# Turning values and keys by VectorE blocks and transfers within SBUF, in a retention and HGRN2 trunk on one core

## The chip, the cores and the metric

The kernel runs on one core of a Trainium2 chip. The metric is the device time of one execution in microseconds (us); with several runs the median is given. A profiled execution gives a trace: every instruction of the engines with its start, its duration and what released it. TensorE (PE) multiplies, with its weight loads (PEld) as a row of their own; VectorE (DVE), ScalarE (ACT) and GpSimd (POOL) do the rest, and SyncE (SP) issues DMAs from one queue that works in order.

## The reference

One decoder layer for 272 prompt positions (16 learned meta tokens and 256 tokens) and 8 decode tokens, 280 columns in all, model width 2048, everything in float32:

```
x <- LN1(alpha*x + 0.5*SwiGLU_1(x))
x <- LN2(alpha*x + (sigmoid(a_r)*o_ret + sigmoid(a_h)*o_hg) @ w_out)
x <- LN3(alpha*x + 0.5*SwiGLU_2(x))

[q_r k_r v_r g_r q_h f i_h g_h a_r a_h] = x @ w_in        # 2048 -> 10*2048
retention, 8 heads of 256:  o = ((q k^T) * D) v + decayed q S,   S_new = gamma^C S + (decayed k)^T v
HGRN2, 16 heads of 128:     o = A v + (q exp(b)) S,              S_new = exp(b_last) S + (k exp(b_last - b))^T v
outputs: y of the 256 tokens and the 8 decode tokens, and the four states
```

The decode tokens use states read from memory; the prompt starts from zero states. What matters here: activations come out of a projection with features on the 128 partitions and time along the row, whereas the products that form a state (k^T v) and the outputs (A v) need values, and for the states keys, with time on the partitions. Those arrays must be turned.

## The kernel before

The program is one long list of matmuls in four stages: the first FFN, the projection stage with the mixer, the output projection, the second FFN. A dense matmul multiplies a 128x128 weight block with 264 to 280 columns in float32r, three times per block (high and low parts of both operands). Weights come in 868 units of 8 blocks: `load` in `stream` issues one 512 KB DMA on SP (tile `raw`, line 185), ScalarE rounds it to `whi` (L188), VectorE subtracts to get `wlo` (L189). All three tiles have three buffers, so a load can be issued as soon as VectorE is through with the unit three places ahead.

The projection stage (`project`) goes over eight head pairs u = 0..7: the six groups f, q_h, i_h, q_r, k_r, v_r of pair u (32 blocks each), then the four gate groups of pair u-1. `evacuate` takes each group out of PSUM. After i_h it starts the generator `mix_hg(u)` (HGRN2, two heads), after v_r the generator `mix_ret(u)` (retention, one head of 256 as two halves c). The generators are advanced by `pump`, once after each k step of a dense group (six matmuls); `yield n` means "go on n steps later". This is how the mixer's own matmuls are placed in TensorE's order, which is written out by hand and is exactly the order of the program. The other engines and SP's queue get their order from a planner at compile time, by priority (the order of the program, weights ahead) and its own estimate of when things are ready; on the chip each works its list in order and waits where something isn't there.

The arrays that are turned, each by TensorE with a 128x128 identity, two blocks b of 128 positions per half or head, into a PSUM bank `pt` or `ptk`, from which ScalarE copies:

- in `mix_hg`: the values `v` of both heads into `vth` (L875, L879), the tile `ends` (first 16 and last 16 columns, L878), read by the state matmuls `pst` (L1024) and the outputs `po` (L1050);
- in `turned(h)` of `mix_hg`: the decayed keys `K` into `kth` (L982, L983), read by `pst`. The loads of the decode state `smh` and values `vbh` of the second head wait for the two `kth` tiles, by a one-column copy on GpSimd (`load`, `values`);
- in `mix_ret`: the values into `vtr` (L1107, L1108), which `split` divides into `vs` (high and low parts), and the rotated keys `k_r` (L1114), which go from PSUM with the decay factors into `ks` (L1129, L1130). `tails` collects the last 24 columns of keys and values and is turned as one block (L1116). `ks` and `vs` are read by the state matmuls `psr` (L1168), `vtr` later by the outputs `por` (L1226) after `centre` has taken off its mean over the 256 features.

`samples(h)` in `mix_hg` updates the decode states on ScalarE and VectorE (L998, L999) and stores them (L1002).

`mix_ret` is started three steps after v_r for all pairs but the second:

```
start(mix_ret(c0 // 2, st["q_r"], st["k_r"], v), 24 if c0 == 2 else 3)
```

The tile `v` has one buffer; `smr` has four, shared by `ks`, `vs` and the decode states of retention.

Of the kernel before, what the change touches and what calls it, by code (L numbers as in the profile page):

```python
# [18 lines left out]
P = 128  # L19
# [109 lines left out]
def trunk(ctx: ExitStack, tc: tile.TileContext, A, O):  # L129
# [417 lines left out]
    with tc.tile_pool(name="yp", bufs=1) as yp:  # L547
# [7 lines left out]
        with tc.tile_pool(name="mp", bufs=1) as mp:  # L555
# [73 lines left out]
            def project(groups):  # L629
                for grp in groups:  # L630
# [4 lines left out]
                    if grp[0] == (QKV_ORDER[0], 0):  # L635
                        outs = norm1.first(block, outs, x0s)
                    elif grp[0] == (QKV_ORDER[2], 0):
                        v = st["i_h"] = tmp("v", (P, 2, T))
                        outs = norm1.second(block, outs, x0s, (v[:, 0, :], v[:, 1, :]))
# [8 lines left out]
            def evacuate(n, c0, c1, o0, o1, b0, b1):  # L648
# [14 lines left out]
                elif n == "i_h":  # L663
                    v = st.pop("i_h", None)
                    if v is None:
                        v = tmp("v", (P, 2, T))
                        nc.scalar.copy(v[:, 0, :], o0)
                        nc.scalar.copy(v[:, 1, :], o1)

                    start(mix_hg(c0 // 2, st["f"], st["k"], st["q"], v), {0: 20, 2: 46}.get(c0, 4))  # L670
                elif n in ("q_r", "k_r"):
                    sc, w, x0 = (1.0, TL, NMETA) if n == "q_r" else (KSC, T, 0)
                    r = tmp(n, (P, 2, w))
                    for j, (a, b, op) in enumerate(((cos, sin, ALU.subtract), (sin, cos, ALU.add))):
# [5 lines left out]
                        nc.vector.tensor_tensor(out=r[:, j, :], in0=r[:, j, :], in1=t, op=op)  # L680
                    st[n] = r
                elif n == "v_r":
                    v = tmp("v", (P, 2, T))
                    nc.scalar.copy(v[:, 0, :], o0)
                    nc.scalar.copy(v[:, 1, :], o1)
                    start(mix_ret(c0 // 2, st["q_r"], st["k_r"], v), 24 if c0 == 2 else 3)
# [24 lines left out]

            NB2 = LP - 2 * P
# [8 lines left out]
            def upper_upper_lower(out, x, at=0):  # L721
# [3 lines left out]
                sub(out[64 : 64 + n], x, out[at : at + n].bitcast(F32))  # L725

# [19 lines left out]
            def mix_hg(u, f, k, q, v):  # L746

                calm = 2
                ends = tmp("ends", (P, 2, 2, NMETA))
                nc.gpsimd.tensor_copy(ends[:, :, 0, :], v[:, :, :NMETA])  # L750
                nc.gpsimd.tensor_copy(ends[:, :, 1, :], v[:, :, T - NMETA :])
# [13 lines left out]
                def load(h):  # L765
# [3 lines left out]
                    nc.gpsimd.tensor_copy(sms[h][:, 0, :1], kts[0][:, 0, :1] if h else acc[:, 15:16])  # L769
                    nc.sync.dma_start(sms[h], A["sg"][2 * u + h])  # L770

                def values(h):
                    nc.gpsimd.tensor_copy(vbs[h][:, 0, :1], kts[1][:, 0, :1] if h else acc[:, 2 * P + 15 : 2 * P + 16])
# [95 lines left out]
                vt = tmp("vth", (P, 2, 2, P))  # L869
                vrow = []  # L870
                for h in range(2):

                    pt = mx_bank("pt")
                    for b in range(2):
                        nc.tensor.transpose(pt[:, b * P : (b + 1) * P], v[:, h, NMETA + b * P : NMETA + (b + 1) * P], ident)  # L875
                    x = pt[:64, 2 * P : 3 * P]
                    if h:
                        nc.tensor.transpose(x, ends.rearrange("p c a t -> p (c a t)"), ident)  # L878
                    nc.scalar.copy(vt[:, h], pt[:, : 2 * P].rearrange("p (b f) -> p b f", b=2))  # L879
                    if h:  # L880
# [95 lines left out]
                def turned(h):  # L976
                    kt = tmp("kth", (P, 2, P), bufs=2)
                    kts.append(kt)
                    pt = mx_bank("ptk")
                    for b in range(2):  # L980
                        t0 = NMETA + b * P
                        nc.tensor.transpose(pt[:, b * P : (b + 1) * P], K[:, h, t0 : t0 + P], ident)  # L982
                    nc.scalar.copy(kt, pt[:, : 2 * P].rearrange("p (b f) -> p b f", b=2))  # L983
# [34 lines left out]
                for h in range(2):  # L1018
# [4 lines left out]
                    for b in range(2):  # L1023
                        nc.tensor.matmul(pst[:, (b + 1) * P : (b + 2) * P], kts[h][:, b, :], vt[:, h, b, :], start=True, stop=True)  # L1024
# [21 lines left out]
                def outputs(h):  # L1046
                    po = mx_bank("po")
                    for b in range(2):
                        o = po[:, b * P : (b + 1) * P]
                        nc.tensor.matmul(o, vt[:, h, b, :], acc[:, (2 * h + b) * P : (2 * h + b + 1) * P], start=True, stop=False)  # L1050
# [26 lines left out]
            def centre(x):  # L1077

                np_, n = x.shape[0], x.shape[1]
                m = tmp("cen", (P, n))[:np_]  # L1080
                nc.vector.tensor_reduce(out=m, in_=x, op=ALU.add, axis=mybir.AxisListType.X)
                nc.vector.tensor_scalar(out=m, in0=m, scalar1=1.0 / 256, scalar2=None, op0=ALU.mult)
                nc.vector.tensor_tensor(out=x, in0=x, in1=m.unsqueeze(2).to_broadcast([np_, n, 256]), op=ALU.subtract)

            def mix_ret(u, q, k, v):
                vt = tmp("vtr", (P, 2, 2, P))

                ks, vs = (tmp(n, (P, 2, 2, 2 * P), dt=F32R, bufs=4, tag="smr") for n in ("ks", "vs"))
# [13 lines left out]
                for i, x in enumerate((k, v)):  # L1102
                    nc.gpsimd.tensor_copy(tails[:, 2 * i : 2 * i + 2, :NB], x[:, :, 2 * P :])
                for c in range(2):
                    pt = mx_bank("pt")
                    for b in range(2):
                        nc.tensor.transpose(pt[:, b * P : (b + 1) * P], v[:, c, b * P : (b + 1) * P], ident)  # L1107
# [4 lines left out]
                    pt = mx_bank("pt")  # L1112
# [264 lines left out]
```

## Time and profile before

| | |
|---|---|
| median of 3 runs | 2566.79 us (2566.35 to 2567.9) |
| profiled execution, span from first to last instruction | 2563.9 us |
| TensorE busy, granted clock | 2553.4 us, 1.000 |
| VectorE busy | 1702.8 us |
| ScalarE busy | 1392.2 us |
| GpSimd busy | 57.0 us |
| DMA engines of SP's queue | 62.0% of 16 engines' span |

The profiled execution's own time is its span; the runs' times hold some 2.9 us more around it. A line of a timeline reads: start, duration, engine, line, operation, output<-inputs, count, and in brackets the idle time before it and what ended that. A line of a group reads: line, engine, operation, shapes, count | busy us, mean ns of one | idle time before them, and what ended it. "L226" or "L240" is the line of a helper that many callers share.

### The profile page before, as it was taken

The page shows a single profiled execution, that of the slowest core. Times are in us where ns is not written, and L with a number is a line of the kernel's source. Part 1 is how long each engine was busy: PE and PEld are TensorE (multiplying, and loading weights), DVE is VectorE, ACT ScalarE, POOL GpSimd, SP SyncE. Part 2 cuts the span into 40 slices and gives each one's busy share as a digit, 9 for nine tenths or more (in the row PEclk, how much of TensorE's full clock was granted, in tenths as well). Part 3 has the DMA queues.
Part 4 walks back from the last instruction along what each step waited for, and adds up shares of the span by engine and source line. Part 5 has one row for each costly group of instructions (what it writes and reads, how often), then busy time and mean ns, then how long its engine had stood idle before and what let it go on. Part 6 is the DMA issues. An engine that isn't in the chain of part 4 may idle for free.

```text
span 2563.9 us, 56275 instructions
## 1 busy us (share of the span) xinstructions
PE 2553.4 (100%) x23424; PEld 2534.4 (99%) x23424; DVE 1702.8 (66%) x2827; ACT 1392.2 (54%) x2186; POOL 57.0 (2%) x152
## 2 busy tenths in 40 slices
PE   9999999999999999999999999999999999999999
PEld 9999999999999999999999999999999999999998
DVE  6444544475569878777777777777885555556555
ACT  5444444444456767767676666675564444444443
POOL 0000000000000000000000000000000000000000
PEclk9999999999999999999999999999999999999999
DMA  7555555555555876767676767675556565565554
GB/s 244 183 187 183 187 182 184 186 182 186 184 201 180 287 265 232 264 214 260 212 264 215 259 223 255 224 239 188 196 190 197 194 197 195 194 196 195 195 195 149
DMA packets 156897, 536.26 MB, mean 209 GB/s; under 512 B 17952, under 2 KB 25952, under 8 KB 156640
## 3 DMA queue, kind: packets, MB, share of 16 engines
q1 hardware_dynamic: 156352, 532.37, 62.0%
q8 instruction: 183, 3.00, 0.5%
q14 instruction: 74, 0.61, 0.1%
q10 hardware_dynamic: 288, 0.29, 0.0%
HBM read 501.99 MB, written 30.61 MB: 208 GB/s over the span
## 4 chain that ended last, share of the span: by engine, by line
PE 96%; DVE 2%; ACT 0%; issue 0%; DMA 0%; SPq 0%; ACTq 0%; DVEq 0%
PE up L218 36%; PE dn L218 19%; PE pj_i_h L218 3%; PE pj_g_r L218 3%; PE pj_q_h L218 3%; PE pj_g_h L218 3%; PE pj_a_r L218 3%; PE pj_a_h L218 3%; PE pj_f L218 3%; PE pj_q_r L218 3%; PE pj_k_r L218 3%; PE wo L218 3%; PE pj_v_r L218 3%; DVE wlo L189 1%; PE pqr L1211 1%; PE psr L1168 0%
## 5 line engine op out<-in xcount | busy, mean ns | idle before, releaser
L189 DVE TENSOR_TENSOR wlo<-raw,whi 128x1024 fp32r<-128x1024 f32 (+1 forms) x869 | 1062.2, 1223 | 740.7 <-ACT whi L188 737.3
L188 ACT CAST whi<-raw 128x1024 fp32r<-128x1024 f32 (+1 forms) x870 | 905.7, 1042 | 909.2 <-PE up L218 411.0
L218 PE MATMUL up<-xh,whi 128*128 128x280 f32 (+1 forms) x2624 | 725.6, 280 | 0.6 <-ACT whi L188 0.6
L218 PE MATMUL up<-xh,wlo 128*128 128x280 f32 (+1 forms) x2624 | 725.8, 280 | 0.4 <-DVE wlo L189 0.3
L218 PE MATMUL up<-xl,whi 128*128 128x280 f32 (+1 forms) x2624 | 725.4, 279 | 0.0
L218 PEld LDWEIGHTS up<-xh,wlo 128*128 128x128 f32 x2624 | 492.6, 189 | 1.0 <-DVE wlo L189 1.0
L218 PEld LDWEIGHTS up<-xh,whi 128*128 128x128 f32 x2624 | 492.6, 189 | 0.8 <-ACT whi L188 0.8
L218 PEld LDWEIGHTS up<-xl,whi 128*128 128x128 f32 x2624 | 492.6, 189 | 0.0
L218 PE MATMUL dn<-hh,whi 128*128 128x280 f32 (+1 forms) x1376 | 384.7, 280 | 0.0
L218 PE MATMUL dn<-hh,wlo 128*128 128x280 f32 (+1 forms) x1376 | 384.3, 279 | 0.0
L218 PE MATMUL dn<-hl,whi 128*128 128x280 f32 (+1 forms) x1376 | 384.3, 279 | 0.0
L218 PEld LDWEIGHTS dn<-hh,whi 128*128 128x128 f32 x1376 | 260.1, 189 | 0.1
L218 PEld LDWEIGHTS dn<-hl,whi 128*128 128x128 f32 x1376 | 260.1, 189 | 0.1
L218 PEld LDWEIGHTS dn<-hh,wlo 128*128 128x128 f32 x1376 | 260.1, 189 | 0.0
L218 PE MATMUL pj_k_r<-xh,whi 128*128 128x280 f32 x256 | 74.2, 290 | 0.0
L218 PE MATMUL pj_g_r<-xh,whi 128*128 128x264 f32 x256 | 74.0, 289 | 0.0
L218 PE MATMUL pj_v_r<-xh,whi 128*128 128x280 f32 x256 | 73.8, 288 | 0.0
L218 PE MATMUL pj_v_r<-xh,wlo 128*128 128x280 f32 x256 | 72.4, 283 | 0.3 <-DVE wlo L189 0.3
L218 PE MATMUL pj_g_h<-xh,whi 128*128 128x264 f32 x256 | 72.7, 284 | 0.0
L218 PE MATMUL pj_k_r<-xh,wlo 128*128 128x280 f32 x256 | 72.4, 283 | 0.0
L218 PE MATMUL pj_v_r<-xl,whi 128*128 128x280 f32 x256 | 72.3, 283 | 0.0
L218 PE MATMUL pj_k_r<-xl,whi 128*128 128x280 f32 x256 | 72.3, 283 | 0.0
(421 smaller groups left out, 5263.4 us busy)
## 6 DMA issues: line engine op xcount, KB each, us to landing
raw<-in_w_up SPq DMA_DIRECT2D x343, 512.0 KB, 4.1
raw<-in_w_in SPq DMA_DIRECT2D x320, 512.0 KB, 4.3
raw<-in_w_dn SPq DMA_DIRECT2D x172, 512.0 KB, 3.5
smr<-in_sr SPq DMA_DIRECT2D x32, 512.0 KB, 5.0
out_srs<-smr SPq DMA_DIRECT2D x32, 512.0 KB, 6.7
raw<-in_w_out SPq DMA_DIRECT2D x32, 512.0 KB, 3.9
vbr<-vrd SPq DMA_DIRECT2D x32, 256.0 KB, 4.1
smh<-in_sg SPq DMA_DIRECT2D x16, 512.0 KB, 5.2
```

Of the source, the lines that this page charges most:

```text
L188: nc.scalar.copy(hi[:, j:jn, :], raw[:, j:jn, :])
L189: nc.vector.tensor_tensor(out=lo[:, j0:j1, :], in0=raw[:, j0:j1, :], in1=hi[:, j0:j1, :].bitcast(F32), op=ALU.subtract)
L218: nc.tensor.matmul(o, w, t, start=start, stop=stop)
L1211: nc.tensor.matmul(pq[32 * j : 32 * j + 32, :256], qdr_at[c][:, 32 * b : 32 * b + 32], sms[2 * e + c][:, j, :], start=e + c == 0, stop=e + ...
```

## The change

The 128 TensorE transposes of `v` (both branches), `k_r` and `K` are replaced. VectorE's `transpose` turns each 32x32 block of a 128x256 operand in place within its 32 partitions, straight from PSUM for i_h and v_r; `pieces` chooses where the blocks lie in the scratch tile. Then `turned_over` moves block (i, j) of a 4x4 grid to (j, i) with 16 DMAs on SP's queue, each of 32 partitions with 512 bytes a row (256 for K). The scratch tile is `v` for i_h, k_r and v_r, and the dead tile `k` for K. The turned tiles are laid out feature by feature with half and block inside (`TURNED`, step of four floats between neighbouring features; `kth` has a step of two).

`evacuate` now fills `ends` and the values' part of `tails` from PSUM by ScalarE, where GpSimd copied them from `v`. `ks` is allocated and filled when k_r is evacuated, and its decay and split read it from SBUF instead of PSUM. `centre` reduces over two dimensions for the new layout. The yields are as before.

```diff
+            TURNED = (P, P, 2, 2)
+            def pieces(z, c):
+                return z[:, :, c].rearrange("p (i f) b -> p b i f", i=4)
+            def turned_over(out, z):
+                z, out = (x.rearrange("p f c b -> p (f c b)") for x in (z, out))
+                n = z.shape[1] // 4
+                for j in range(4):
+                    for i in range(4):
+                        nc.sync.dma_start(
+                            out[32 * j : 32 * j + 32, n * i : n * (i + 1)], z[32 * i : 32 * i + 32, n * j : n * (j + 1)])
...
                 elif n == "i_h":
-                    v = st.pop("i_h", None)
-                    if v is None:
-                        v = tmp("v", (P, 2, T))
-                        nc.scalar.copy(v[:, 0, :], o0)
-                        nc.scalar.copy(v[:, 1, :], o1)
+                    ends = tmp("ends", (P, 2, 2, NMETA))
+                    vt = tmp("vth", TURNED)
+                    v = tmp("v", TURNED)
+                    for j, o in enumerate(st.pop("i_h", (o0, o1))):
+                        nc.vector.transpose(pieces(v, j), o[:, NMETA:LP])
+                        nc.scalar.copy(ends[:, j, 0, :], o[:, :NMETA])
+                        nc.scalar.copy(ends[:, j, 1, :], o[:, T - NMETA : T])
+                    turned_over(vt, v)
...
+                    if n == "k_r":
+                        st["ks"] = ks = tmp("ks", (P, 2, *TURNED[1:]), dt=F32R, bufs=4, tag="smr")
+                        z = tmp("v", TURNED)
+                        for j in range(2):
+                            nc.vector.transpose(pieces(z, j), r[:, j, : 2 * P])
+                        turned_over(ks[:, 1].bitcast(F32), z)
...
                 elif n == "v_r":
-                    v = tmp("v", (P, 2, T))
-                    nc.scalar.copy(v[:, 0, :], o0)
-                    nc.scalar.copy(v[:, 1, :], o1)
+                    vt = tmp("vtr", TURNED)
+                    v = tmp("v", TURNED)
+                    for j, o in enumerate((o0, o1)):
+                        nc.vector.transpose(pieces(v, j), o[:, : 2 * P])
+                        nc.scalar.copy(tails[:, 2 + j, : T - 2 * P], o[:, 2 * P :])
+                    turned_over(vt, v)
...
                 def turned(h):
-                    kt = tmp("kth", (P, 2, P), bufs=2)
+                    kt = tmp("kth", (P, P, 1, 2), bufs=2)
                     kts.append(kt)
-                    pt = mx_bank("ptk")
-                    for b in range(2):
-                        t0 = NMETA + b * P
-                        nc.tensor.transpose(pt[:, b * P : (b + 1) * P], K[:, h, t0 : t0 + P], ident)
-                    nc.scalar.copy(kt, pt[:, : 2 * P].rearrange("p (b f) -> p b f", b=2))
+                    z = k[:, h, : 2 * P].rearrange("p (f c b) -> p f c b", c=1, b=2)
+                    nc.vector.transpose(pieces(z, 0), K[:, h, NMETA:])
+                    turned_over(kt, z)
...
                 for c in range(2):
-                    pt = mx_bank("pt")
+                    f = slice(c * P, (c + 1) * P)
                     for b in range(2):
-                        nc.tensor.transpose(pt[:, b * P : (b + 1) * P], v[:, c, b * P : (b + 1) * P], ident)
-                    nc.scalar.copy(vt[:, :, c, :], pt[:, : 2 * P].rearrange("p (b f) -> p b f", b=2))
-                    f = slice(c * P, (c + 1) * P)
-                    split(vs[:, 0, :, f], vs[:, 1, :, f], vt[:, :, c, :])
+                        split(vs[:, 0, b, f], vs[:, 1, b, f], vt[:, :, c, b])
                     yield 1
-                    pt = mx_bank("pt")
-                    for b in range(2):
-                        nc.tensor.transpose(pt[:, b * P : (b + 1) * P], k[:, c, b * P : (b + 1) * P], ident)
...
-                    todo = [(pt[:, b * P : (b + 1) * P], dec[:, b, u : u + 1], [ks[:, 0, b, f]], 0, ks[:, 1, b, f]) for b in range(2)]
+                    todo = [(ks[:, 1, :, c, b].bitcast(F32), dec[:, b, u : u + 1], [ks[:, 0, :, c, b]], 0, ks[:, 1, :, c, b]) for b in range(2)]
```

More of the change, by code (lines that the diff above doesn't have):

```diff
@@ L637, in project @@
                     elif grp[0] == (QKV_ORDER[2], 0):
-                        v = st["i_h"] = tmp("v", (P, 2, T))
-                        outs = norm1.second(block, outs, x0s, (v[:, 0, :], v[:, 1, :]))
+                        first = st["i_h"] = [tmp("rot") for _ in range(2)]
+                        outs = norm1.second(block, outs, x0s, first)
                     else:
@@ L1023, in mix_hg @@
                     for b in range(2):
-                        nc.tensor.matmul(pst[:, (b + 1) * P : (b + 2) * P], kts[h][:, b, :], vt[:, h, b, :], start=True, stop=True)
+                        nc.tensor.matmul(pst[:, (b + 1) * P : (b + 2) * P], kts[h][:, :, 0, b], vt[:, :, h, b], start=True, stop=True)
                     nc.scalar.copy(S[:, 0, :], pst[:, :P])
@@ L1133, in mix_ret @@
                 alone(qdr, q)
-                vts = [vt[:, 0], vt[:, 1], vs2]
+                vts = [[vt[:, :, c, b] for c in range(2)] for b in range(2)] + [[vs2[:, c, :] for c in range(2)]]
                 vrow = rows_out(vt2.rearrange("p c f -> p (c f)")[16:24, :], 256, "vr")
```

45 lines of the change are left out of this document (18 added, 27 removed).

## The prediction, made before the changed kernel ran

> **What bounds the kernel now.** I read the page first: the share of each engine and the chain that ended last.
>
> ```profile
> span 2563.9 us, 56275 instructions
> ...
> PE 2553.4 (100%) x23424; PEld 2534.4 (99%) x23424; DVE 1702.8 (66%) x2827; ACT 1392.2 (54%) x2186; POOL 57.0 (2%) x152
> ...
> PE 96%; DVE 2%; ACT 0%; issue 0%; DMA 0%; SPq 0%; ACTq 0%; DVEq 0%
> ```
>
> TensorE is busy for all but 10.5 us, and 96% of the chain is its matmuls. So a matmul taken out is time won, one for one, as long as its queue, which runs in a fixed order, never comes upon an operand that isn't there. The change can lose only in that second way. It acts in the projection stage alone, so I read that stage by stretches next (columns: length, then busy time of PE, weight loads, DVE, ACT, POOL, then granted clock, DMA share, GB/s):
>
> ```profile
> 793.00:1712.00 919.00, 916.89 (x9355) 901.75 (x9354) 737.20 (x1502) 623.95 (x1190) 54.42 (x121) 1.00 0.71 242
> ```
>
> TensorE is full here too, at clock 1.00. VectorE is 80% busy, ScalarE 68%.
>
> **The gain: 128 transposes leave TensorE.** The groups by line, with their counts:
>
> ```profile
> L1107 PE MATMUL pt<-ident,v 128*128 128x128 f32 x32 | 6.2, 276 | 0.0
> L982 PE MATMUL ptk<-ident,K 128*128 128x128 f32 x32 | 6.1, 273 | 0.0
> L1114 PE MATMUL pt<-ident,k_r 128*128 128x128 f32 x32 | 6.1, 273 | 0.0
> L875 PE MATMUL pt<-ident,v 128*128 128x128 f32 x32 | 6.1, 273 | 0.0
> ```
>
> The 273 ns is one instruction's latency; matmuls overlap, so the price is the pitch. It comes from the order in time around one pair:
>
> ```profile
> 1159.53 0.28 PE L218 MATMUL pj_a_r<-xh,wlo 128*128 128x264 f32 x1
> 1159.64 0.38 PE L1107 MATMUL pt<-ident,v 128*128 128x128 f32 x2
> 1159.78 0.36 PE L218 MATMUL pj_g_r<-xh,whi 128*128 128x264 f32 x1
> 1159.98 0.28 PE L218 MATMUL pj_g_r<-xl,whi 128*128 128x264 f32 x1
> ```
>
> A dense matmul takes 0.11 us of the order (1159.53 to the pair at 1159.64). From 1159.53 to 1159.98 are 0.45 us, two dense matmuls and two transposes: 0.112 us each, so a transpose takes as long as a dense matmul of 264 columns. 128 x 0.112 = **14.4 us won**. The small transposes of ends, tails and meta stay.
>
> **ScalarE and VectorE.** Per head pair ScalarE loses ten copies of 256 or 280 columns and gains some small ones: a relief, beside the path. VectorE gains 8 turns per head pair, 64 in all. No turn stands in the trace; the nearest rows are its elementwise operations on 128x256 at 0.42 us (below), so 64 x 0.42 = 27 us on an engine with 182 us idle in the stage. I take nothing for them except where a chain waits for them; with the four smaller subtractions of vs in place of two, an upper bound is 1 us per pair where VectorE is behind, 8 us; the lower bound is 0.
>
> **The transfers.** One `turned_over` issues 16 DMAs on SP's queue, and a head pair has five of them (i_h, k_r, v_r, and K once per head): 80 per pair, 640 in all. SP's queue works in order and also carries every weight load. Its rows in the steady pair u=3, from K to the state matmuls:
>
> ```profile
> 1141.67 0.38 SPq L770 DMA_DIRECT2D smh<-in_sg  x1
> 1144.33 0.33 SPq L185 DMA_DIRECT2D raw<-in_w_in  x1
> 1144.71 0.42 SPq L774 DMA_DIRECT2D vbh<-vh1d  x1
> 1147.48 6.99 SPq L185 DMA_DIRECT2D raw<-in_w_in  x3
> 1154.67 0.34 SPq L1002 DMA_DIRECT2D out_sgs<-smh  x1
> 1157.14 0.33 SPq L185 DMA_DIRECT2D raw<-in_w_in  x1
> 1157.92 0.34 SPq L1002 DMA_DIRECT2D out_sgs<-smh  x1
> 1158.82 1.17 SPq L1030 DMA_DIRECT2D out_sgp<-Sh  x2
> 1160.21 0.62 SPq L185 DMA_DIRECT2D raw<-in_w_in  x1
> 1162.40 0.29 SPq L730 DMA_DIRECT2D vrd<-vt  x1
> 1163.11 0.33 SPq L185 DMA_DIRECT2D raw<-in_w_in  x1
> 1164.42 0.80 SPq L1156 DMA_DIRECT2D vbr<-vrd  x2
> ```
>
> An issue takes 0.29 us even for the 4 KB of vrd, and one right behind another starts 0.38 us later (1144.33 to 1144.71). No row shows a transfer of 32 partitions within SBUF; bounds are 0.29 and 0.42 us, and I take 0.36, between vrd's 0.29 plus a gap of 0.05 and the raw pitch of 0.38. Sixteen cost SP 5.8 us. That is harmless in sum (640 x 0.36 = 230 us of 919) but not where four bursts follow each other.
>
> The other ends of the chain (VectorE, ScalarE and TensorE in time; then a row of the queue's waits, and group rows with the mean ns of one):
>
> ```profile
> 1138.42 0.42 DVE L240 TENSOR_TENSOR K<-K,T 128x256 f32<-128x256 f32 x1
> 1147.85 0.45 DVE L680 TENSOR_TENSOR k_r<-k_r,rot 128x280 f32<-128x280 f32 x1
> 1157.46 0.39 ACT L684 COPY v<-pj_v_r 128x280 f32<-128x280 f32 x1 [0.26 <-PE pj_v_r L218]
> 1168.74 0.50 PE L1168 MATMUL psr<-vs,ks 128*128 128x256 f32 x3
> ```
>
> ```profile
> SPq L1156 <- DMA vrd<-vt: 11.8, 8, 2.5
> L226 DVE TENSOR_TENSOR vs<-vtr,vs 128x256 fp32r<-128x256 f32 x16 | 6.7, 420 | 4.3 <-ACT vs L225 4.3
> L1130 DVE SCALAR_TENSOR_TENSOR ks<-pt,dec,ks 128x128 fp32r<-128x128 f32 x32 | 11.2, 349 | 1.0 <-ACT ks L1129 0.3
> ```
>
> Now the chain of the values of retention, for that pair. K is final at 1138.8; its first turn ends at 1139.3. Both K bursts: 32 x 0.36 = 11.5 us, with some six other issues at 0.38 between (2.3): SP is through at 1153.1. Only then comes the burst of k_r, ready since 1149: 5.8 us, a raw and an out_sgs: 1159.6. A small transfer takes 2.0 us to land (vrd issued at 1162.40, the vbr that waits for it goes at 1164.42), so 1161.6. The turn of v_r, whose projection is ready at 1157.46, writes the same scratch tile "v" that these transfers read, and there is one buffer: two turns, 0.84, to 1162.5. Its burst, with a raw and a store, 6.5 us: 1169.0; landed 1171.0. Then vs is split in four pieces on ScalarE and VectorE, about 0.35 each, overlapped: 1.7 us, 1172.7. Behind it TensorE's psr now stands at 1168.74 less the 12 transposes removed since 1139: 1167.4. **It waits 5.3 us**, and everything behind it in the fixed order waits too. That is so for the pairs 2 to 7, six times: 32 us. Pair 0 has no K bursts ahead of its values, and pair 1's generator starts 24 steps late by the code: 0 for both.
>
> The same working with an issue every 0.29 us ends at 1168.1, a wait of 0.7 us (4 in all); with 0.42 it ends at 1176.4, a wait of 9.0 us (54).
>
> Elsewhere the bursts are covered: vth is first read some 45 steps later; K's turns land at about 1155, as the state matmuls start; weight loads put off by one burst lose 5.8 less the 2.8 us between two of them, 3.0 us, and the cover is there:
>
> ```profile
> ACT whi L188 <- DMA raw<-in_w_in: 40.7, 27, 3.1
> ```
>
> A cast has waited up to 3.1 us for its load without TensorE idling. If that cover is gone, the excess is TensorE's.
>
> **Sum.** 2563.9 - 14.4 + 32 = 2581.5 us of span. The median shown, 2566.79, lies 2.9 above the profiled span: **2584 us**. This likeliest case by itself runs from 2566.8 - 14.4 + 4 = 2556 to 2566.8 - 14.4 + 54 = 2606.
>
> **The rivals.**
> *All hidden (faster).* If the small issues are far cheaper than vrd's 0.29, or vs comes in time, only the gain remains: 2566.8 - 14.4 = 2552. For it: SP has room in the sum. Against: 64 transfers and 15 other issues between 1139.3 and 1167.4, with two landings of 2.0, need even at 0.29 a little more than there is.
> *Even.* A wait of 2.4 us, six times, eats the 14.4: 2567. An issue every 0.32 us would do that.
> *Blocked order (much slower).* The loads of vbh(1) now wait for K's second transfers:
>
> ```profile
> DMA to landing us min/median/max: 6.1/6.6/7.0
> 1154.03 1.92 DVE L999 SCALAR_TENSOR_TENSOR smh<-vbh,meta,smh 128x128 f32<-128x128 f32 x7
> ```
>
> Kt landed at 1154, vbh issued between 1154.5 and 1160 (behind k_r's burst), 6.6 us to land: the second head's samples on VectorE can't go before 1161 to 1167, where they went at 1154. If they stand ahead of v_r's turns in VectorE's order, the burst starts at 1164 to 1170 and psr waits 7 to 13 us; with 10, 6 x 10 - 14.4: 2612. The order decides, which the trace of before can't show.
> *Clock falls in the gaps.* TensorE idles 2.1 us in the whole stage now (919.00 less 916.89), and its clock is 1.00; a wait of 5.3 us is new to it. If the clock then fell to half for as long as the wait had lasted, each wait would lose 2.65 us more, 16 in all: 2600. For it speaks no row, since none has such a gap. The Trainium skill, "TensorE: Matmul & The Clock Gate", Part 1, has this rule: after an idle window of about 3.4 us the clock is halved until as much busy time has passed; an estimate from that page is 1.7 us for each wait, 10 in all, 2594. No run here shows it yet, and a wait below its window would cost nothing more.
> *Strided operands.* The matmuls concerned:
>
> ```profile
> L1168 PE MATMUL psr<-vs,ks 128*128 128x256 f32 x112 | 15.1, 275 | 0.0
> L1226 PE MATMUL por<-dtab,vtr 128*128 128x256 f32 (+1 forms) x64 | 13.5, 333 | 0.0
> L1050 PE MATMUL po<-acch,vth 128*128 128x128 f32 x64 | 12.3, 274 | 0.0
> L1024 PE MATMUL pst<-vth,kth 128*128 128x128 f32 x64 | 9.8, 287 | 0.0
> ```
>
> 288 of them (96 of psr's). If each lost another pitch of 0.112: 32 us on top, 2616. No row has a stationary operand whose neighbouring columns lie 16 bytes apart, as ks and vt will have; the nearest are these same matmuls on dense columns, so I take 0. The Trainium skill, "SBUF — State Buffer", Door 1, says that each access that crosses to a new 16-byte line pays a penalty, which would make it this case; no run shows it so far.
>
> **How the numbers follow.** Likeliest 0.36, blocked order 0.16, clock 0.08, strided 0.06: slower, 0.66 in all; what of the likeliest's own range lies below 2572 is counted under the next two. Hidden, or nearly so, 0.24: faster. Even 0.10: same. 0.2%, 5 us, is about what a measurement of this kernel can tell from no change. The range reaches from 2553, which keeps half of the hidden case, to 2616, which leaves half of the blocked one out.
>
> **What would show it.** Right: no L875, L982, L1107, L1114 on TensorE; bursts of 16 issues at about 0.36 us; TensorE idle before psr, about 5 us in each of six pairs, released by vs; k_r's burst behind K's. Wrong: an issue of 0.1 us, or psr without idle time (hidden); idle before dense matmuls released by wlo (blocked order); a granted clock below 1.00 (clock); por, po or pst longer than their rows (strided).

## The result and the profile after

The changed kernel takes 2857.18 us (median, 2850.55 to 2859.13), the kernel before 2566.57 in the same runs: a ratio of 1.1126, interval 1.111 to 1.1141. It is 290 us slower, where 17 were forecast. The profiled execution spans 2854.3 us. The page after, its first lines, the granted clock in 40 slices and the shares of the chain that ended last:

```profile
span 2854.3 us, 57043 instructions
...
PE 2626.3 (92%) x23296; PEld 2598.6 (91%) x23296; DVE 1739.6 (61%) x2907; ACT 1389.0 (49%) x2172; POOL 25.1 (1%) x128
...
PEclk9999999999989998989989798998999999999999
...
PE 80%; DMA 6%; SPq 5%; DVE 4%; issue 2%; ACT 2%; POOL 0%; DVEq 0%; ACTq 0%; POOLq 0%
```

128 matmuls are gone, and yet TensorE is busy for 73 us more than before. It also idles: its gaps above 0.3 us, added up from the trace, are 218.7 us, where before they were 2.6. The loss is these two numbers: 216 + 73 = 289. All of it lies in the projection stage, whose row was 919 us at clock 1.00 before (stretch, its length, PE busy, clock, DMA share, GB/s):

```profile
793.00:2005.00 1212.00, 992.38 (x9252) 0.90 0.61 192
```

The waits, summed (us in total, times, longest):

```profile
PE pst L1038 <- DMA kth<-k: 91.6, 14, 11.8
PE pt L1124 <- ACT tails L695: 75.2, 8, 15.3
PE psr L1176 <- ACT vs L225: 27.1, 8, 4.6
ACT ks L1137 <- DMA ks<-v: 53.4, 8, 10.9
DVE v L694 <- DMA ks<-v: 43.6, 8, 9.7
```

TensorE waits at three places, `pst`, `tails` and `psr`: 105, 75 and 29 us, and in all eight pairs. Pair u=4 in time, selected rows (SPq is SP's queue, L749 a transfer of `turned_over`):

```profile
1409.53 0.77 DVE L996 STREAM_TRANSPOSE k<-K 128x256 f32<-128x256 f32 x2
...
1419.87 0.66 DVE L687 STREAM_TRANSPOSE v<-k_r 128x256 f32<-128x256 f32 x1
...
1427.76 10.78 SPq L749 DMA_DIRECT2D kth<-k  x16
1429.19 1.15 PE L1038 MATMUL pst<-vth,kth 128*128 128x128 f32 x4 [3.82 <-DMA kth<-k]
1439.84 6.85 SPq L749 DMA_DIRECT2D ks<-v  x11
1440.04 1.24 PE L1038 MATMUL pst<-vth,kth 128*128 128x128 f32 x4 [9.59 <-DMA kth<-k]
1453.38 0.93 ACT L1137 ACTIVATE ks<-ks,dec 128x128 fp32r<-128x128 f32 x2 [6.01 <-DMA ks<-v]
1453.39 1.08 DVE L694 STREAM_TRANSPOSE v<-pj_v_r 128x256 f32<-128x256 f32 x2 [4.76 <-DMA ks<-v]
1454.21 0.16 ACT L695 COPY tails<-pj_v_r 128x24 f32<-128x24 f32 x1
1454.50 7.48 SPq L749 DMA_DIRECT2D vtr<-v  x12
1455.00 0.45 PE L1124 MATMUL pt<-ident,tails 128*128 128x128 f32 x1 [8.60 <-ACT tails L695]
1463.52 2.41 SPq L749 DMA_DIRECT2D vtr<-v  x4
1467.70 1.37 ACT L225 CAST vs<-vtr 128x128 fp32r<-128x128 f32 x4 [2.12 <-DMA vtr<-v]
1468.80 0.50 PE L1176 MATMUL psr<-vs,ks 128*128 128x256 f32 x1 [3.52 <-ACT vs L225]
```

K is turned at 1410.3, but the second head's transfers go out until 1438.5 and TensorE stands before `pst` for 9.6 us. k_r was turned at 1420.5; its transfers come behind K's. Only when they have landed may v_r's turn write the scratch tile (1453.39); the `tails` copy goes with it, and TensorE waits another 8.6 us. Then `vtr` goes out, and `psr` waits. Sixteen issues in a row took 10.78 us: 0.67 each, where the prediction took 0.36.

The clock in that pair, around its gaps:

```profile
1429.00:1440.00 11.00, 1.26 (x5) 0.52 0.30 97
1440.04:1443.18 3.14, 3.14 (x14) 0.50 0.61 188
1443.18:1446.32 3.14, 3.14 (x28) 1.00 0.10 26
1455.00:1465.00 10.00, 10.00 (x62) 0.74 0.21 52
```

In the gap of 9.6 us the clock falls to half (0.52 over the first stretch). Behind the gap TensorE is busy throughout: for 3.14 us at half its clock, with 14 matmuls, and then at full clock, with 28 matmuls in the same time. Over the whole trace neighbouring dense matmuls start 0.22 us apart at half clock and 0.113 at full clock (medians). Behind the next gap, of 8.6 us, the clock is 0.74 over 10 us. That agrees with the rule of the Trainium skill, "TensorE: Matmul & The Clock Gate", Part 1, that an idle window of about 3.4 us halves the clock until TensorE has been busy again. Added up over the trace, the clock stands at half during 116 us of TensorE's busy time. At half the rate, as measured above, that is an estimated 58 us of work lost; before the change it was none.

### The profile page after: what moved, and what is told of

It reads as the page before. It is cut to its first block, busy times and chain, and to the rows that moved or that the text cites. A ratio compares the mean times of both kernels' runs of the same rounds, so it can differ in the third digit from the quotient of the medians.

```text
span 2854.3 us, 57043 instructions
## 1 busy us (share of the span) xinstructions
PE 2626.3 (92%) x23296; PEld 2598.6 (91%) x23296; DVE 1739.6 (61%) x2907; ACT 1389.0 (49%) x2172; POOL 25.1 (1%) x128
## 4 chain that ended last, share of the span: by engine, by line
PE 80%; DMA 6%; SPq 5%; DVE 4%; issue 2%; ACT 2%; POOL 0%; DVEq 0%; ACTq 0%; POOLq 0%
PE up L218 33%; PE dn L218 17%; SPq L749 4%; PE pj_q_h L218 3%; PE wo L218 3%; PE pj_i_h L218 3%; PE pj_q_r L218 3%; PE pj_f L218 3%; DMA raw<-in_w_in 2%; PE pj_g_r L218 2%; PE pj_k_r L218 2%; PE pj_g_h L218 2%; PE pj_a_r L218 2%; PE pj_a_h L218 2%; DVE wlo L189 2%
## 5 line engine op out<-in xcount | busy, mean ns | idle before, releaser
L1038 PE MATMUL pst<-vth,kth 128*128 128x128 f32 x64 | 19.4, 438 | 104.8 <-DMA kth<-k 91.6
L1038 PEld LDWEIGHTS pst<-vth,kth 128*128 128x128 f32 x64 | 14.2, 283 | 107.5 <-issue 88.0
L218 PE MATMUL pj_g_r<-xh,wlo 128*128 128x264 f32 x256 | 76.7, 300 | 6.1 <-DVE wlo L189 6.1
L218 PE MATMUL pj_g_r<-xl,whi 128*128 128x264 f32 x256 | 76.6, 299 | 0.0
L218 PE MATMUL pj_a_r<-xh,whi 128*128 128x264 f32 x256 | 76.0, 297 | 0.0
```

The source lines that it names most:

```text
L218: nc.tensor.matmul(o, w, t, start=start, stop=stop)
```

## The experiments

All but the issue measurement were timed against the kernel before. "Idle" is the sum of TensorE's gaps above 0.3 us, "busy" TensorE's busy time. The theory: SP's queue, at twice the price taken, makes the turned tiles late; the strided operands and the clock add to it. The rival: the order, in which work stands behind other work whatever an issue costs.

| kernel | median us | ratio, interval | idle us | busy us |
|---|---|---|---|---|
| changed | 2857.2 | 1.1126 [1.111, 1.1141] | 218.7 | 2626.3 |
| s1_strided | 2603.0 | 1.014 [1.0123, 1.0157] | 5.7 | 2587.3 |
| e1_later | 2801.2 | 1.0912 [1.0896, 1.0928] | 168.4 | 2619.0 |
| e2_dense | 2849.1 | 1.1098 [1.1082, 1.1115] | 232.9 | 2608.7 |
| e3_dram | 2726.9 | 1.0626 [1.061, 1.0642] | 119.2 | 2601.1 |
| e5_twov | 2865.9 | 1.1159 [1.1142, 1.1176] | 246.9 | 2608.4 |
| e6_tails | 2871.4 | 1.1186 [1.1171, 1.1201] | 257.2 | 2609.5 |
| p_ret | 2720.5 | 1.0601 [1.0585, 1.0617] | 112.7 | 2600.3 |
| e7_pool | 2771.8 | 1.0801 [1.0783, 1.0819] | 140.5 | 2619.7 |
| e9_fill | 2875.3 | 1.1204 [1.1187, 1.1221] | 132.8 | 2729.4 |
| e4_all | 2690.6 | 1.0482 [1.0467, 1.0498] | 102.4 | 2577.0 |
| e11_pool16 | 2695.2 | 1.0491 [1.0475, 1.0507] | 98.1 | 2588.6 |
| e10_pool_dram | 2639.5 | 1.0286 [1.0272, 1.03] | 52.1 | 2575.1 |
| c_ihk | 2616.1 | 1.0189 [1.0175, 1.0203] | 35.1 | 2567.6 |
| c_ih | 2567.6 | 1.0002 [0.9993, 1.001] | 3.7 | 2552.5 |
| c_ih_pool | 2567.3 | 1.0001 [0.9992, 1.0009] | 3.5 | 2552.1 |
| c_ih_own | 2567.4 | 1.0001 [0.9992, 1.0009] | 4.5 | 2553.4 |
| c_ih_from2 | 2565.4 | 0.9995 [0.9986, 1.0004] | 5.8 | 2552.2 |

**The layout alone (s1_strided).** The kernel before, with the changed layout and nothing else:

```diff
-                vt = tmp("vth", (P, 2, 2, P))
+                vt = tmp("vth", (P, P, 2, 2)).rearrange("p f c b -> p c b f")
... kth, vtr and ks in the same way
```

> The kernel before with one part of the change: vth, kth, vtr and ks get the changed kernel's layout (neighbouring columns 16 bytes apart, 8 for kth); TensorE still does all the turns, no transfer is added. Theory that strided stationary operands cost TensorE time: their weight loads go from 191 to about 320 ns, each of the 288 matmuls loses about 0.08 to 0.12 us, 23 to 35 us in all, so 2590 to 2601, with clock 1.00 and no new idle time. Rival, the longer rows of the changed kernel are latency that lies under other matmuls: 2567, within 0.2%. Second rival, they were long in the changed kernel only because its clock was lower: the rows here are back at 191 and 274 ns, 2567.

2603.0 us, 36 more than before and 2 above the first theory's range. The group rows (PEld is the load of the stationary operand), first of the kernel before, then of this one:

```profile
L1050 PEld LDWEIGHTS po<-acch,vth 128*128 128x128 f32 x64 | 9.7, 191 | 0.0
L1024 PEld LDWEIGHTS pst<-vth,kth 128*128 128x128 f32 x64 | 8.4, 192 | 0.0
```

```profile
L1050 PEld LDWEIGHTS po<-acch,vth 128*128 128x128 f32 x64 | 17.4, 320 | 0.0
L1024 PEld LDWEIGHTS pst<-vth,kth 128*128 128x128 f32 x64 | 12.0, 208 | 0.4
L1024 PE MATMUL pst<-vth,kth 128*128 128x128 f32 x64 | 17.1, 413 | 0.0
```

A stationary operand with a step of 16 bytes loads in 320 ns instead of 191; `kth`, with a step of 8, in 208 instead of 192. As the moving operand, `vth` at 16 bytes makes `pst` 413 ns (287 before). Busy time rises by 33.9 us, 0.118 for each of the 288 matmuls. The Trainium skill, "SBUF — State Buffer", Door 1, wants two hits on each 16-byte line for full speed; the step between 8 and 16 bytes agrees.

**What an issue costs (m1_issue).** Extra transfers behind the end of the kernel before:

```diff
+        blocks(nc.sync, t("m_shift"))      # 16 transfers of 32 partitions, as in the change
...
+        for k in range(16):
+            nc.sync.dma_start(t(f"m_full{k}"), z)
...
+        blocks(nc.gpsimd, t("m_pool"))
```

> The kernel before, with extra transfers behind its last output (they belong to no output): eight groups of 16, the source written by VectorE from the last tile. On SP: blocks of 32 partitions with 512 bytes a row from one group of partitions to another, as in the change (tile m_shift); the same within the same partitions (m_same); with four pieces of 128 bytes a row (m_piece); all 128 partitions with 2 KB a row within SBUF (m_full), and to DRAM (md); DRAM to 32 partitions (m_back); then as the first on ScalarE's queue (m_act) and on GpSimd's (m_pool). Theory: an issue has a fixed price of some 0.3 us on SP, and the 0.51 to 0.59 us (pitch 0.64) of the change's transfers is what any transfer within SBUF pays: m_shift, m_same, m_piece and m_full about 0.55 to 0.65, md and m_back 0.3 to 0.45. Rival, the price goes with the partitions or bytes: m_full above m_shift. Second rival, it was high only beside the busy engines: all 0.3 here. On ScalarE the same as on SP, on GpSimd over 0.8.

The timeline of the issues (16 of each):

```profile
2574.09 10.08 SPq L1276 DMA_DIRECT2D m_same<-mz  x16
2584.22 10.32 SPq L1283 DMA_DIRECT2D m_piece<-mz  x16
2594.59 10.38 SPq L1285 DMA_DIRECT2D m_full<-mz  x16
2605.01 9.42 SPq L1287 DMA_DIRECT2D md<-mz  x16
2614.47 7.89 SPq L1291 DMA_DIRECT2D m_back<-md  x16
2562.75 8.00 POOL L1276 DMA_DIRECT2D m_pool<-mz  x16 [796.39 <-ACT y L463]
```

Within SBUF an issue costs 0.63 to 0.65 us in a row, be it 32 partitions or 128, one piece or four; m_shift, beside ScalarE's issues, 0.69; ScalarE 0.69 too. To DRAM it is 0.59, from DRAM 0.49, on GpSimd 0.50. So the first theory holds for the price within SBUF; md came out far above the 0.3 to 0.45 expected, and GpSimd far below 0.8. The 0.29 to 0.42 of the rows before were single issues from and to DRAM.

**Dense columns (e2_dense).**

```diff
-            TURNED = (P, P, 2, 2)
+            TURNED = (P, 2, 2, P)
```

> The changed kernel with dense columns in vth, kth, vtr, ks and the scratch tiles (half, block, feature): each of the same 16 transfers now moves four pieces of 128 bytes a row (two for K) in place of one of 512. Theory of strided operands: weight loads of psr, po, por back at about 191 ns, TensorE's busy time falls by 20 to 30 us, the waits before pst, tails and psr stay: 2825 to 2840. If an issue costs more for more pieces, the waits grow by as much as the issue: at 0.9 in place of 0.6 us, 80 x 0.3 = 24 us a pair, up to 100 to 190 us more. Rival (strides don't matter): 2857.

Eight us less, not 20 to 30: busy time falls by 17.6, while idle time rises by 14. `po` and `por` load in 191 and 190 ns again, `psr` and `pst`, which stand behind the gaps, still in 287 and 289. So the strides cost the changed kernel less than the 34 us of s1_strided.

**Fewer issues (e3_dram), later readers (e1_later).**

```diff
-                        nc.sync.dma_start(out[32*j ...], z[32*i ...])   # 16 of them
+                nc.sync.dma_start(scr, z)                               # DRAM
+                    nc.sync.dma_start(out[32*j ...], back[j])           # 4 of them
```

> The changed kernel with the 16 transfers of a turn replaced by five: the scratch tile goes out to DRAM in one transfer of 128 partitions and comes back in four, each with 32 partitions of the turned tile; layout and order are the same. Theory that SP's issue time is what makes the tiles late: 200 issues in place of 640, a turn takes 5 x 0.4 to 0.6 = 2 to 3 us of SP in place of 10, against some 2 us more to land twice; TensorE's idle time falls from 216 to 30 to 90 us and the clock rises, 2620 to 2720. Rival, order: what waits stands behind others in the order of ScalarE, VectorE and SP whatever an issue costs: over 2800.

130 us less, with 100 us of idle time gone: the price matters, but half the idle time stays (`psr` 75, `pst` 39), and the time lies a little above the theory's range.

```diff
-                    start(mix_ret(...), 24 if c0 == 2 else 3)
+                    start(mix_ret(...), 24)
+                yield (6, 8, 25)[min(u, 2)]      # ahead of pst, taken off the yield behind it
```

> The changed kernel with its readers put later in TensorE's order: mix_ret starts 24 steps after v_r in every pair (3 before), and the state matmuls pst stand 6, 8 or 25 steps later (pairs 0, 1, others), taken off the yield behind them. Theory that the turned tiles only come too late for a fixed place: TensorE's idle time of 216 us falls below 40, the granted clock goes back to 0.99 or more, and what stays is 2567 - 14 + 20 to 30 for strided operands: 2575 to 2620. Rival, SP's queue has no room for 640 small transfers, so the weights come late instead: idle time moves to the dense matmuls (released by wlo) and the time stays over 2750.

Neither in full: the time is the rival's (over 2750), the place of the waits is not. 168 us of idle time stay, few of them before dense matmuls, most again before `tails` (82), `pst` (37) and `psr` (32). SP's queue, in time, shows why:

```profile
1391.09 0.33 SPq L185 DMA_DIRECT2D raw<-in_w_in  x1
1391.46 1.77 SPq L749 DMA_DIRECT2D kth<-k  x3
1393.94 0.33 SPq L185 DMA_DIRECT2D raw<-in_w_in  x1
1394.37 1.77 SPq L749 DMA_DIRECT2D kth<-k  x3
```

The turn's transfers stand between weight loads. A load waits until its buffer is free, one unit of TensorE's work, some 2.8 us; so three transfers go out per load, and K's 32 take from 1389.4 to 1423.9. When TensorE runs on, the turns take as much longer as their readers were put off.

**The tails wait (e5_twov, e6_tails).** One gives v_r's turn a scratch tile of its own, the other copies the tails ahead of the turn:

```diff
-                    v = tmp("v", TURNED)
+                    v = tmp("v2", TURNED, tag="on_r", bufs=2)      # e5_twov
```

> The changed kernel with a scratch tile of its own for the turn of v_r (another tile's buffer), so that this turn does not wait for k_r's transfers. Theory that the tails wait (75 us) is the chain k_r's transfers, scratch free, turn of v_r, tails copy: it falls below 15 us, but vtr's transfers stand behind ks in SP's queue all the same, so that psr waits instead; 30 to 60 us less, 2800 to 2830. Rival, the tails copy stands behind the ks activations on ScalarE: the wait stays and the time is within 10 us of 2857.

> The changed kernel with the two copies of the values' tails put ahead of the turns of v_r in the program, nothing else. Theory that the copy is held up by the turn: the tails wait of 75 us falls below 15, psr waits in its place (29 grows to 70 to 90): 2825 to 2850. Rival, ScalarE's order holds it (ks activations ahead of it): unchanged, 2857. If the tails alone were late and nothing behind them, 75 us and some clock would come back: 2765 to 2780.

In e6_tails the lines that copy `tails` stand in a loop of their own ahead of the turns. The waits, first of e5_twov, then of e6_tails:

```profile
PE psr L1176 <- ACT vs L225: 124.7, 8, 16.4
ACT tails L695 <- DVE v L694: 19.4, 15, 2.0
```

```profile
PE psr L1177 <- ACT vs L225: 134.2, 8, 19.4
ACT tails L694 <- PE pj_v_r L218: 10.9, 6, 1.8
```

The wait before `tails` went, 75 us to 9 and to 0.5, and the one before `psr` rose from 29 to 125 and 134. Both kernels are slower than the changed one by 9 and 14 us. The three waits are one lateness; who stands first in TensorE's order shows it. That `psr` takes it over was expected, the gain was not there. Why the three waits together grew, from 209 us to 239 and 245, no run shows.

**The retention alone (p_ret).** The values and K of HGRN2 stay on TensorE, with the code of before.

> The kernel before with the retention's part of the change alone: k_r and v_r turned by VectorE and 32 transfers a pair, in the change's layout; the values and K of HGRN2 stay on TensorE. Theory that the lateness is the sum of the bursts ahead in SP's queue: without K's 32 transfers (20 us a pair) and i_h's 16, k_r's burst starts as soon as it is turned, the waits before tails and psr together fall from 104 us to below 30, and the time is 2567 - 7.2 (64 transposes) + 20 (160 strided matmuls at 0.125) + waits = 2580 to 2610. Rival, the retention's own chain (k_r's 16, scratch free, v_r's turn, its 16, landing, split) is longer than its place allows whatever stands ahead: tails and psr wait 60 to 110 us, 2640 to 2710.

The rival, a little above its range: 2720.5 us. Without K's and i_h's bursts ahead, TensorE waits 53 us before `tails` and 52 before `psr`, as many together as with them:

```profile
PE pt L1133 <- ACT tails L693: 52.9, 7, 11.1
PE psr L1185 <- ACT vs L225: 51.5, 8, 7.2
```

In one pair its chain, k_r turned at 1351.25, `ks` out until 1364.25, v_r turned at 1368.2, `vtr` out until 1382.1, `psr` at 1385.6, takes 34 us; before, from k_r ready (1148.3) to `psr` (1168.74) were 20.

**Another queue (e7_pool), busy gaps (e9_fill).**

```diff
-                        nc.sync.dma_start(
+                        nc.gpsimd.dma_start(
```

> The changed kernel with its 640 small transfers issued from GpSimd's queue (pitch 0.49 us in the measurement of issues, where SP's was 0.64) in place of SP's; weight loads alone with the stores on SP as before the change. Theory that what counts is one queue for weights and turns: K(1)'s burst, stretched by loads that wait for wlo, goes through in 8 us, TensorE's idle time falls from 216 to 60 to 130 us, 2690 to 2770. Rival, the four bursts still follow each other in one queue and the copies that hold back smh and vbh stand between them on GpSimd: idle time 180 or more, 2810 to 2900.

85 us less, 78 of them idle time; as the theory had it, just above its upper edge. But two things changed at once: the queue is no longer shared with the weights, and an issue is cheaper, 0.50 us in a row where SP took 0.64. For the 64 transfers of K, k_r and v_r the second is 9 us a pair, 72 in eight (an estimate from m1_issue), so this run alone does not tell the two apart. The Trainium skill, "DMA: Bandwidth & Descriptors", Issuing engines are not separate DMA queues, says that issuing from several engines saves only the time of the issue, which is usually small beside the transfer; here it is not small, since 64 issues stand one behind the other in the chain.

```diff
+                    for _ in range(60 if h else 16):
+                        nc.tensor.transpose(pst[:, 0:P], ident, ident)
... and 60 ahead of the tails transpose
```

> The changed kernel with dummy transposes of the identity on TensorE just ahead of the late readers, 16 before the first head's pst, 60 before the second's and 60 before tails, into the PSUM area that the real operation then overwrites: 136 x 0.112 = 15 us of work a pair inside 27 us of waits. Theory that the granted clock falls after idle time and that this makes some 50 us of the 290 lost (290 = 216 idle - 14 + 36 strided + about 53 left over): the mean clock rises from 0.958 towards 0.98 and the time falls by 20 to 35 us although TensorE does 1088 transposes more: 2820 to 2838. Rival, what is left over is not the clock: no gain, 2857, or more by what the dummies exceed a wait.

18 us slower: the clock rose as the theory had it (0.958 to 0.978 over the span), the time went the rival's way. The stage's row, where the changed kernel had 0.90:

```profile
793.00:2020.00 1227.00, 1093.81 (x10325) 0.95 0.60 189
```

The parts: 1088 dummies x 0.112 = 122 us of work, but busy time rises only by 103, so the rest of the work became 19 us cheaper. Idle time fell by 86, not 122: the dummies outlasted some waits. The clock record agrees: at half during 83 us of busy time, an estimated 41 us lost, 17 fewer than the changed kernel's 58. Busy time grew by 73 us although 14 us of transposes are gone, so 87 us have to be explained. The clock accounts for some 58 and the strides for 18 (e2_dense) to 34 (s1_strided), 76 to 92 together; no third cause of that size is left.

**All mends (e4_all), and off SP's queue (e11_pool16, e10_pool_dram).** e4_all is later readers, dense columns and five transfers through DRAM on SP.

> The changed kernel with three mends together: readers later (as in e1_later), dense columns (as in e2_dense), and a turn by one transfer to DRAM and four back (as in e3_dram). Theory that issue time, place and stride are all there is: idle time below 20 us, clock 0.99 or more, 2567 - 14 + 0 to 25 = 2553 to 2578. Rival, the waits of the DRAM version before psr (75 us, from the chain k_r, scratch, v_r) outlast the 14 us by which mix_ret goes later: 2610 to 2680.

The rival, a little above its range: 2690.6, with 65 us before `psr`. In one pair (selected rows of VectorE and SP):

```profile
1364.87 0.44 DVE L694 STREAM_TRANSPOSE v<-pj_v_r 128x256 f32<-128x256 f32 x1
...
1368.03 1.99 SPq L185 DMA_DIRECT2D raw<-in_w_in  x2
...
1375.43 0.33 SPq L185 DMA_DIRECT2D raw<-in_w_in  x1
...
1378.22 1.28 SPq L748 DMA_DIRECT2D turn<-v  x1
```

v_r is turned at 1365.3 and its first transfer issued at 1378.2, behind `ks` and five weight loads. What is left in this pair is the order of SP's queue more than the price. The next two put the transfers on GpSimd's queue, 16 within SBUF or five through DRAM, with an own scratch tile, dense columns and later readers.

> The changed kernel with dense columns, readers later (as in e1_later), a scratch tile of its own for v_r (as in e5_twov), and the 16 transfers of each turn on GpSimd's queue; nothing goes through DRAM. Theory that the order of SP's queue (transfers of a turn between weight loads that TensorE's progress releases) is what keeps the tiles late: on GpSimd a turn takes 16 x 0.49 = 8 us from the moment its operand is there, four in a row 31 us of a pair's 61, and the readers come 14 to 17 us later than before: idle time below 40 us, 2560 to 2610. Rival, the number of transfers in one queue counts whichever it is: K(1) still ahead of k_r ahead of v_r, idle time 80 us or more, over 2650.

> As e11_pool16, with a turn by one transfer to DRAM and four back in place of the 16, also on GpSimd's queue. Theory of SP's order: 5 x 0.5 = 2.5 us of issue and two landings of some 2 us, 7 us a turn, no weight load between; nothing waits any more: idle time below 10 us, clock 1.00, 2552 to 2562, faster than the kernel before. Rival, issue price or landing: as e4_all, which had the same transfers on SP, 2691, or within 30 us of it.

The waits before `pst`, `tails` and `psr` are gone (0.6 us in e11_pool16). Of e10_pool_dram:

```profile
L1179 PE MATMUL psr<-vs,ks 128*128 128x256 f32 x112 | 15.1, 275 | 0.0
L1041 PE MATMUL pst<-vth,kth 128*128 128x128 f32 x64 | 10.2, 296 | 0.0
```

So it was SP's order that kept the tiles of e4_all late, and not the price: a transfer back from DRAM took 0.66 to 0.83 us on GpSimd's queue in e10_pool_dram (medians by tile), and 0.57 to 0.60 on SP's in e4_all. The own scratch tile is new too, but in the pair shown v_r's turn waited 2.9 us for the tile and its transfers 13 us for the queue. The times are still not the theory's: 98 and 52 us of idle time stand elsewhere now, most of it before dense matmuls. Of e11_pool16:

```profile
ACT smh L1011 <- POOL meta L1003: 90.3, 8, 13.4
PE pj_g_h L218 <- ACT whi L188: 49.7, 10, 9.1
```

ScalarE waits for `meta`, a copy that stands behind the transfers in GpSimd's order (1229.3 in one pair, between those of `ks` and `vtr`), and the weight casts stand behind ScalarE's wait. Their place suggests that the one causes the other; no run took the copy out.

**Is any part worth it? (c_ih, c_ih_pool, c_ih_own, c_ih_from2, c_ihk)** c_ih turns only HGRN2's values, into dense columns, by 16 transfers on SP; c_ih_pool has them on GpSimd; c_ih_own a scratch tile of its own; c_ih_from2 leaves pairs 0 and 1 as before; c_ihk turns the values and K, both through DRAM on GpSimd, with `pst` later.

```diff
+                    if c0 >= 4:                       # c_ih_from2; the others always
+                        nc.vector.transpose(pieces(v, j), o[:, NMETA:LP])
...
+                        turned_over(vt, v)
```

> The kernel before with the values of HGRN2 (i_h) alone turned by VectorE, into dense columns (four pieces of 128 bytes a row for each of 16 transfers); keys, k_r and v_r stay on TensorE. vth is first read some 45 steps later, so theory: its 16 issues of about 0.6 us fall between weight loads and are covered; 32 transposes x 0.112 us = 3.6 us won, 2563. Rival, a burst puts weight loads off by up to 10 us and the casts come late: idle time before dense matmuls of 2 to 5 us in each pair, 2580 to 2605.

> As c_ih (the values of HGRN2 alone turned by VectorE, dense columns, rest as before the change), with its 16 transfers on GpSimd's queue. c_ih won 0.44 us in each later pair (4 transposes x 0.11) and lost 3.2 us once, in the first pair, where a tile came late. Theory that the loss came of SP's queue: it goes away, 32 x 0.112 = 3.6 us won, 2563 to 2564. Rival, the loss came of VectorE's or ScalarE's order in the first pair: stays at 2567.

> As c_ih (the values of HGRN2 alone, 16 transfers on SP's queue, dense columns), with a scratch tile of its own (a buffer that on_r leaves free) in place of v, which the retention's values also use. In c_ih and c_ih_pool alike TensorE idled 2.0 us once, in the first pair, before the transposes of the retention's values (pt<-ident,v), whichever queue the transfers were on. Theory that the copy of those values waited there for i_h's transfers to leave the shared tile: the gap goes, 32 x 0.112 = 3.6 us won, 2563 to 2564, just faster than the kernel before (0.14%). Rival, the gap is VectorE's or ScalarE's order: 2567 as before.

> As c_ih_own, but only in the pairs 2 to 7; pairs 0 and 1 turn their values on TensorE as before. In c_ih_own the first pair's gap of 2.0 us stayed, so the shared tile was not its cause; the trace shows the copy of the retention's values there behind Qm copies on ScalarE that wait for VectorE, and the dense matmuls come 0.44 us earlier in each later pair. Theory that 0.112 us a transpose is real and nothing else happens in the pairs 2 to 7: 24 x 0.112 = 2.7 us won, span 2561.2 against 2563.9, median 2564.2, ratio 0.999. Rival, a new order elsewhere eats it as it did in the first pair: 2566 to 2570.

> The HGRN2 part of the change alone (i_h and K; k_r and v_r stay on TensorE), with all mends: dense columns, one transfer to DRAM and four back on GpSimd's queue, an own scratch tile, pst later by 6, 8 or 25 steps. Theory that with the retention's chain away nothing waits: 64 transposes x 0.112 = 7.2 us won, 2560 to 2563. Rival, what is left in e10_pool_dram (52 us of idle before dense matmuls, weights cast late) came of pst's and the samples' new place, not of the retention: 10 to 40 us lost, 2575 to 2610.

The four that turn the values alone are level with the kernel before. The starts of the same dense matmuls in both traces show what happens in c_ih: from the third on each pair gains some 0.44 us (four transposes, 0.11 each), and the first loses 3.2. There TensorE stands once (of c_ih_own):

```profile
819.33 0.44 PE L1113 MATMUL pt<-ident,v 128*128 128x128 f32 x2 [2.00 <-ACT v L686]
```

The copy of the retention's values on ScalarE comes 1.6 us later than before, behind `Qm` copies that wait for VectorE, which now has two turns more. The theory of the shared scratch tile fell: a tile of its own left the gap as it was. c_ih_from2, which leaves the first two pairs on TensorE, has no such gap. It is 0.9 us below the kernel before in the median, with 1 inside the interval of the ratio, so the expected 2.7 is not shown; in its profiled execution TensorE's idle time is 3.2 us above the kernel before, in other small waits. c_ihk loses 49 us, a little more than its rival had, with 35 us of idle time, nearly half of it before `pj_g_r`, whose `wlo` comes late. No version beats the kernel before by more than the measurement can tell.

## Why the prediction was wrong

- **The price of an issue** is the step that failed first. The prediction took 0.36 us, between 0.29 and 0.42, from rows of transfers from and to DRAM. In the changed kernel one took 0.51 to 0.59 us, and in a row one went out every 0.64 (m1_issue) to 0.67. The prediction's own chain with 0.64 (K's bursts through at 1162.1, k_r's at 1173.0, v_r turned at 1175.9, its burst through at 1186.8) ends at 1190.5 in place of 1172.7: a wait of 23 us a pair in place of 5.3, 185 in eight pairs. Measured are 209 before `pst`, `tails` and `psr`. It was said that no row shows such a transfer; then the bounds should not have been closed at the nearest rows.
- **"K's turns land at about 1155, as the state matmuls start", at nothing**, and the bursts "covered": with 0.64 this margin was gone. `pst` waited 105 us.
- **"0 for both"** pairs 0 and 1: all eight wait. p_ret shows that the retention's chain is too long by itself, even without K's bursts ahead of it.
- **The queue's order.** The working let loads slip between the bursts as single issues. They wait for TensorE and hold the transfers behind them (e1_later, e4_all). The rival of blocked order named VectorE and the loads of `vbh`; the order that the traces show is SP's.
- **Strided operands, taken at 0**: 33.9 us of busy time in s1_strided, near the rival's 32, and 18 in e2_dense. **The clock**: its rival came true as well, for some 58 us. Both were treated as cases that exclude one another, and they add up.
- **The sum with what was measured**: 2566.8 - 14.4 + 216 (idle time) + 58 (clock) + 18 to 34 (strides) = 2844 to 2860, where 2857 was measured and 2584 forecast. How much of the 209 us of waits is the price and how much the order of the queue is not separated.
- **Right**: the direction; k_r's burst behind K's; 0.112 us a transpose (0.11 in c_ih); the turns on VectorE, 0.43 to 0.65 us each, hidden but for the first pair (c_ih).

## What to carry to other kernels

Before work is moved into many small transfers, measure or bound generously what one issue of just that kind costs, and multiply by the longest chain, not by the total. A transfer in a queue with demand-paced loads goes at the pace of the loads, so a turn needs a queue whose other work does not wait. When one lateness shows at several waits of an engine with a fixed order, taking the first away moves it to the next; and rivals that act on different resources add up.

## What was not expected of the hardware

- An issue on SP within SBUF costs the same for 32 and 128 partitions (0.63 and 0.65 us in a row), more than from DRAM (0.49). Within SBUF GpSimd issues faster than SP, every 0.50 us; back from DRAM slower, 0.66 to 0.83 us against 0.57 to 0.60 (e10_pool_dram, e4_all).
- At half the granted clock TensorE does half the work: 14 matmuls in 3.14 us, and 28 in the next 3.14 us at full clock.
- A step of 8 bytes costs a stationary operand next to nothing (208 against 192 ns), a step of 16 bytes 129 ns more.
- VectorE's turn of 128x256 takes 0.43 to 0.45 us into a tile with a step of 4 or 8 bytes, 0.61 to 0.65 with a step of 16.
